# Decoder step with split float32 weights: both parts kept in DRAM after their first use

## The chip, the cores and the metric

The kernel runs on one core of a Trainium2 chip. The metric is the device time of one execution in microseconds (us). TensorE does the matmuls, VectorE (DVE) and ScalarE (ACT) the element-wise work, GpSimd (POOL) a few small operations, and SyncE (SP) issues most DMAs. Every engine works through its own queue in order, and the engines wait for one another through semaphores.

## What is computed

One inference step of a one-layer hybrid decoder on a prompt of 2048 tokens and a sample group of 8 x 8 tokens, model width 1024. Cut to what matters:

```python
h = rmsnorm(x, norm1_g)
z = h @ w_in                                   # 1024 x 4352: r, k, v, low-rank columns, pooling branch, two gates
a = up_a(rwkv7(shifted z))                     # recurrence over tokens, 8 heads x 64
b = up_b(pool(z))                              # causal means over 2, 4, 8, 16 tokens
x = x + (sig(gate_a) * a + sig(gate_b) * b) @ w_o
h = rmsnorm(x, norm2_g)
x = x + square(relu(h @ w_ff1)) @ w_ff2        # 1024 -> 4096 -> 1024
y = rmsnorm(x, final_norm_g)
```

The inputs, the weights and the result are float32; the states of the recurrence, the shift and the pooling are outputs as well.

## The kernel before

**Split products.** A float32 product is made of three float32r matmuls. A weight w is split into hi, its float32r rounding, and lo = w - hi; the activations are split in the same way, and hi x hi, lo x hi and hi x lo are added up in one PSUM tile (`products`).

**Blocks and stages.** The 2112 tokens are cut into five blocks of 384, 448, 448, 448 and 384 columns, the sample group in the fourth. A block goes through three stages: A (the input projection, matmuls named pi and pv), M (the up projections pab and the output projection po) and F (the feed-forward, in 8 groups of 512 hidden columns, named pf and p). The constant ORDER sets how stages of the blocks follow each other: A0 A1 A2 M0 A3 F0 M1 A4 F1 M2 F2 M3 F3 M4 F4. The recurrence runs beside them in 16 sub-steps of 128 tokens (names k0 to k15) and one for the samples (k16): chains of small matmuls, VectorE and GpSimd operations and DMA round trips that are mixed into the matrix work.

**Units of weights.** `load_unit` (line 156) fetches 512 KB of weights, 128 partitions x 1024 values, enough for 24 matmuls. There are 34 units in an A stage, 16 in an M stage and 64 in an F stage (in each group four of w1, then four of w2), 114 a block and 570 in all. A unit has a raw tile (two buffers), and tiles for hi and for lo (three buffers each). SP's queue issues the load into raw (line 164), ScalarE casts raw to hi (166), VectorE subtracts (167). A raw tile is free when VectorE has read it, a hi or lo tile when TensorE has done the unit's last matmul.

In stage F the second product goes in an order of its own: three quarters of w2's first two units, then the last quarters of these, then units three and four. So the unit that takes over the tile of w2's first unit, w2's fourth, follows close behind it: of the 96 matmuls of a group's second product, the first unit's last is number 42 and the fourth unit's first is number 73. In stage M the output projection does the same once: the first unit's last is number 45 and the fourth's first is number 73.

**Order.** TensorE's order is written out: `TensorOrder` chains every matmul to the one before it. The order on the other engines comes from a scheduler at build time, which places the instructions by their dependences and priorities. A queue never overtakes: what waits at its head holds all that is behind it. SP's queue also has at most eight DMAs under way, since a DMA waits for the eighth before it.

**GpSimd** has little: the powers behind the RMS norms (rs, line 181; rt, line 785, from which VectorE makes the tiles md that TensorE needs), the state product of the recurrence (spk, 1283), the group norm's scale (sm), small fills, and the DMAs of the constants in the first 60 us and of the sample states (sld).

Of the kernel before, what the change touches and what calls it, by code (L numbers as in the profile page):

```python
# [12 lines left out]
F32 = mybir.dt.float32  # L13
F32R = mybir.dt.float32r
AF = mybir.ActivationFunctionType
ALU = mybir.AluOpType
# [4 lines left out]
P = 128  # L21
# [46 lines left out]
def hybrid_step(ctx: ExitStack, tc: tile.TileContext, a: dict, outs: list):  # L68
# [11 lines left out]
    V, S, G, D = nc.vector, nc.scalar, nc.gpsimd, nc.sync  # L80

    cp = ctx.enter_context(tc.tile_pool(name="cp", bufs=1))
    dr = ctx.enter_context(tc.tile_pool(name="dr", bufs=1, space=DRAM))
    wp = ctx.enter_context(tc.tile_pool(name="wp", bufs=3))
# [69 lines left out]

    T = TensorOrder()

    def load_unit(parts, shape, name):
        raw = wp.tile([P, 1024], F32, tag="raw", name=name + "r", bufs=2)
        hi = wp.tile([P, 1024], F32R, tag="whi", name=name + "h")
        lo = wp.tile([P, 1024], F32R, tag="wlo", name=name + "l")  # L160
        used = 0
        for src in parts:
            k, n = src.shape[1], src.shape[2]
            D.dma_start(out=raw[:, used:used + k * n].rearrange("p (k n) -> p k n", k=k), in_=src)
            used += k * n
        S.copy(hi[:, :used], raw[:, :used])  # L166
        V.tensor_tensor(lo[:, :used], raw[:, :used], hi[:, :used], op=ALU.subtract)  # L167
        r = lambda t: t[:, :used].rearrange("p (k n) -> p k n", n=shape[1])
        return r(hi), r(lo)

# [136 lines left out]
    for job in h_jobs(0):  # L307
        job()
    dg0 = diagonals(r1_of[0], tok_tiles(0), "r1d0")
    pre = {m: load_unit([w_in[:, :, m * P:(m + 1) * P]], (8, P), f"wi0_{m}") for m in (12, 13)}  # L310

    consts = ExitStack()
# [12 lines left out]
    for dst, vec in ((muv, a["mu_shift"][2 * DA:3 * DA]), (lng, a["ln_x_g"]), (lnb, a["ln_x_b"])):  # L325
        for e in range(2):
            G.dma_start(out=dst[e * 64:e * 64 + 64],
                        in_=vec.rearrange("(q e i) -> e q i", e=2, i=HD)[e].unsqueeze(0).to_broadcast([64, NPAIR, HD]))
# [64 lines left out]
    for e in range(2):  # L393
        G.dma_start(out=vsd[:, 0, e * 256:(e + 1) * 256].rearrange("s (q i) -> s q i", i=HD),
                    in_=a["state_shift"][:, 2 * DA:3 * DA].rearrange("s (q e i) -> e s q i", e=2, i=HD)[e])
# [55 lines left out]
    def col_tile(b, hs, m, evac):  # L451
        g0, n, s = blocks[b]
        wu = (pre.pop(m, None) if b == 0 else None) or load_unit([w_in[:, :, m * P:(m + 1) * P]], (8, P), f"wi{b}_{m}")
        ps = mm_ps(f"pi{b}_{m}")
        yield from gemm(ps[:, :n + s], products(wu, hs, range(8), n + s))
        if b not in rrow:
            h_rows(b, None if b else dg0)
        evac(n + s, ps)
# [38 lines left out]
    def values(b, hs):  # L497
# [5 lines left out]
        for q in range(4):  # L503
            wu = load_unit([w_in[:, 2 * q:2 * q + 2, 2 * DA:3 * DA]], (2, DA), f"wv{b}_{q}")
            for (o, sz, kind, src) in tiles:
                if q == 0:
                    pss[o] = (mm_ps, wk_ps)[len(pss) // 3](f"pv{b}_{o}")
                for kk in range(2):
                    k = 2 * q + kk
                    for i, (x, w) in enumerate(((hs[0], wu[0]), (hs[0], wu[1]), (hs[1], wu[0]))):  # L510
                        T.matmul(pss[o][:sz, :], col(x, k, o, sz), w[:, kk, :], start=(k == 0 and i == 0), stop=(k == 7 and i == 2))
                        yield
# [481 lines left out]
    for i in range(2):  # L994
        t = dr.tile([32, 32, 32], F32, name=f"dxf{i}")
# [511 lines left out]
```

## Time and profile before

| | |
|---|---|
| time, median of 3 runs (lowest to highest) | 3177.41 us (3175.01 to 3185.4) |
| the profiled execution | 3178.24 us |
| its span, first to last instruction | 3176.5 us |
| busy: TensorE, VectorE, ScalarE, GpSimd | 97%, 65%, 40%, 5% |
| granted TensorE clock, mean | 0.99 of 2.4 GHz |
| DMA: moved, mean rate | 462 MB, 146 GB/s |
| DMA queues: share of the DMA engines' time | SP 50.3%, GpSimd 0.2% |

The stages, by the first and last matmul that carries their names, lie at these times of the span: A0 27 to 191 us, A1 to 407, A2 to 617, M0 to 706, A3 to 915, F0 to 1246, M1 to 1343, A4 to 1522, F1 to 1886, M2 to 1982, F2 to 2380, M3 to 2483, F3 to 2815, M4 to 2888, F4 to 3140.

How to read it: a row of the windows view gives a stretch's length, and for each engine the busy time and in brackets its instructions; PEclk is the clock that TensorE was granted, 1.00 for 2.4 GHz and 0.50 for 1.2 GHz; then the mean busy share of the 16 DMA engines and what they moved. A row of the waits view names an engine and its instruction, and behind the arrow what ended its wait. Idle time of an engine that is not the bound costs nothing.

### The profile page before, as it was taken

Reading aid. Unit: us, or ns where it says so; the run is one execution under the profiler, and the core shown is the slowest. Engines: PE = TensorE matmul, PEld = TensorE weight load, DVE = VectorE, ACT = ScalarE, POOL = GpSimd, SP = SyncE. Lnnn points to the kernel's source line nnn. Section 1 sums busy time; section 2 is a strip of 40 time slices with the busy share of each in tenths; the row PEclk is TensorE's granted clock in tenths of the full one; section 3 lists DMA queues with packets and bytes.
Section 4 is the critical chain, followed back from the end, with each engine's and each line's share of the span. In section 5 each row is a group of like instructions: output and inputs, shape, how many; then the busy total and the mean of one; then the engine's idle time right before and its main releaser. Section 6 shows DMA issues by size and latency. Waiting matters only on the chain.

```text
span 3176.5 us, 55187 instructions
## 1 busy us (share of the span) xinstructions
PE 3077.0 (97%) x21869; PEld 2816.8 (89%) x21869; DVE 2060.8 (65%) x3992; ACT 1256.4 (40%) x2108; POOL 158.8 (5%) x361
## 2 busy tenths in 40 slices
PE   7999999899999999999999999999999999999997
PEld 7898888888899999898988889888898899999997
DVE  5757666586748667775757668557668654466554
ACT  5444433353333434543443434333334333344333
POOL 4000000000100000010000000000001000000000
PEclk9999999999999999999999999999999999999999
DMA  7756665564544455655544356334446444364443
GB/s 219 204 155 177 187 173 147 152 164 134 146 133 130 127 144 160 200 166 145 159 118 116 114 146 183 102 89 130 125 118 198 108 122 121 107 209 133 120 133 106
DMA packets 738662, 462.24 MB, mean 146 GB/s; under 512 B 143649, under 2 KB 715467, under 8 KB 738396
## 3 DMA queue, kind: packets, MB, share of 16 engines
q1 hardware_dynamic: 737476, 457.55, 50.3%
q8 instruction: 172, 2.82, 0.4%
q0 software_dynamic: 928, 1.16, 0.2%
q14 instruction: 86, 0.70, 0.1%
HBM read 388.81 MB, written 65.54 MB: 143 GB/s over the span
## 4 chain that ended last, share of the span: by engine, by line
PE 76%; DVE 9%; DMA 8%; issue 2%; SPq 2%; ACT 2%; POOL 1%; DVEq 0%; POOLq 0%; ACTq 0%
PE pf L150 20%; PE p L150 20%; PE pi L150 16%; PE po L150 5%; PE pab L150 3%; PE pv L150 3%; DMA pin<-pd 1%; DMA gm<-gd 1%; DMA lin<-zd 1%; SPq L1171 0%; PE gT L150 0%; DVE acc L914 0%; SPq L1167 0%; PE k16py L150 0%; DMA out<-xo 0%
## 5 line engine op out<-in xcount | busy, mean ns | idle before, releaser
L914 DVE TENSOR_TENSOR acc<-p,acc 128x448 f32<-128x448 f32 (+1 forms) x320 | 181.1, 591 | 164.2 <-PE p L150 163.7
L852 DVE SCALAR_TENSOR_TENSOR rl<-pf,rsc 128x448 f32<-128x448 f32 (+1 forms) x160 | 94.8, 594 | 163.7 <-PE pf L150 162.8
L166 ACT CAST w_3h<-w_3r 128x1024 fp32r<-128x1024 f32 x80 | 84.1, 1051 | 284.7 <-PE p L150 150.0
L166 ACT CAST w_1h<-w_1r 128x1024 fp32r<-128x1024 f32 x80 | 84.0, 1050 | 234.3 <-DMA w_1r<-in_w_ff 102.9
L166 ACT CAST w_2h<-w_2r 128x1024 fp32r<-128x1024 f32 x80 | 84.0, 1050 | 160.0 <-PE pf L150 81.3
L167 DVE TENSOR_TENSOR w_1l<-w_1r,w_1h 128x1024 fp32r<-128x1024 f32 x80 | 97.8, 1222 | 58.8 <-ACT w_1h L166 58.6
L166 ACT CAST w_0h<-w_0r 128x1024 fp32r<-128x1024 f32 x80 | 84.2, 1052 | 102.0 <-PE pf L150 75.8
L150 PE MATMUL p<-gh,w_2h 128*128 128x448 f32 (+1 forms) x320 | 114.9, 359 | 8.6 <-DVE acc L914 8.6
L150 PE MATMUL p<-gh,w_1h 128*128 128x448 f32 (+1 forms) x320 | 114.0, 356 | 2.2 <-ACT gs L717 2.2
L150 PE MATMUL p<-gh,w_0h 128*128 128x448 f32 (+1 forms) x320 | 114.3, 357 | 0.3 <-ACT gh L855 0.3
L150 PE MATMUL p<-gl,w_2h 128*128 128x448 f32 (+1 forms) x320 | 114.3, 357 | 0.0
L150 PE MATMUL p<-gh,w_2l 128*128 128x448 f32 (+1 forms) x320 | 114.1, 356 | 0.0
L150 PE MATMUL p<-gl,w_3h 128*128 128x448 f32 (+1 forms) x320 | 113.5, 355 | 0.0
L150 PE MATMUL p<-gh,w_3h 128*128 128x448 f32 (+1 forms) x320 | 113.5, 355 | 0.0
L150 PE MATMUL p<-gh,w_3l 128*128 128x448 f32 (+1 forms) x320 | 113.4, 354 | 0.0
L150 PE MATMUL p<-gh,w_1l 128*128 128x448 f32 (+1 forms) x320 | 113.3, 354 | 0.0
L150 PE MATMUL p<-gh,w_0l 128*128 128x448 f32 (+1 forms) x320 | 113.0, 353 | 0.0
L150 PE MATMUL p<-gl,w_1h 128*128 128x448 f32 (+1 forms) x320 | 112.9, 353 | 0.0
L167 DVE TENSOR_TENSOR w_2l<-w_2r,w_2h 128x1024 fp32r<-128x1024 f32 x80 | 97.7, 1222 | 22.5 <-ACT w_2h L166 22.2
L150 PE MATMUL p<-gl,w_0h 128*128 128x448 f32 (+1 forms) x320 | 107.1, 355 | 3.9 <-DVE gl L857 3.9
L167 DVE TENSOR_TENSOR w_3l<-w_3r,w_3h 128x1024 fp32r<-128x1024 f32 x80 | 97.5, 1219 | 17.6 <-ACT w_3h L166 17.6
L167 DVE TENSOR_TENSOR w_0l<-w_0r,w_0h 128x1024 fp32r<-128x1024 f32 x80 | 97.6, 1220 | 13.8 <-ACT w_0h L166 13.5
(3861 smaller groups left out, 9810.5 us busy)
## 6 DMA issues: line engine op xcount, KB each, us to landing
w_0r<-in_w_ff SPq DMA_DIRECT2D x80, 512.0 KB
w_1r<-in_w_ff SPq DMA_DIRECT2D x80, 512.0 KB
w_2r<-in_w_ff SPq DMA_DIRECT2D x80, 512.0 KB
w_3r<-in_w_ff SPq DMA_DIRECT2D x80, 512.0 KB
gd<-gt SPq DMA_DIRECT2D x48, 224.0 KB
gm<-gd SPq DMA_DIRECT2D x48, 224.0 KB
gf<-in_final_norm_g SPq DMA_DIRECT2D x36, 256.0 KB
out<-xo SPq DMA_DIRECT2D x15, 512.0 KB
```

The source lines that it names most:

```text
L150: self.issue(nc.tensor.matmul(out, lhsT, rhs, start=start, stop=stop), cost)
L166: S.copy(hi[:, :used], raw[:, :used])
L167: V.tensor_tensor(lo[:, :used], raw[:, :used], hi[:, :used], op=ALU.subtract)
L852: V.scalar_tensor_tensor(rl[:, :nt], ps[:, :nt], 0.0, rs, op0=ALU.max, op1=ALU.mult)
L914: V.tensor_tensor(acc[:, m, :nt], pss[m][:, :nt], acc[:, m, :nt], op=ALU.add)
```

## The change

`load_unit` keeps a table, `split`, of units that it has met. The key is the unit's name without its block number, so all five blocks share an entry. At a unit's first use (all 114 units of block 0) the load and the split stay, and two DMAs on SP's queue write hi and lo to two new DRAM tensors, 128 rows of 4 KB each. For the 456 units of the later four blocks, nothing is cast or subtracted and no raw tile is taken: GpSimd's queue loads hi and lo from those DRAM tensors straight into the tiles, two DMAs of 512 KB. The DRAM tensors are float32 and the tiles float32r, so these loads convert the type.

```diff
+    split = {}
+
     def load_unit(parts, shape, name):
-        raw = wp.tile([P, 1024], F32, tag="raw", name=name + "r", bufs=2)
+
+        key = name.split("_", 1)[1] + name[:2]
         hi = wp.tile([P, 1024], F32R, tag="whi", name=name + "h")
         lo = wp.tile([P, 1024], F32R, tag="wlo", name=name + "l")
-        used = 0
-        for src in parts:
-            k, n = src.shape[1], src.shape[2]
-            D.dma_start(out=raw[:, used:used + k * n].rearrange("p (k n) -> p k n", k=k), in_=src)
-            used += k * n
-        S.copy(hi[:, :used], raw[:, :used])
-        V.tensor_tensor(lo[:, :used], raw[:, :used], hi[:, :used], op=ALU.subtract)
+        used = sum(src.shape[1] * src.shape[2] for src in parts)
+        both = [(hi, "h"), (lo, "l")]
+        if key in split:
+            for (t, x), d in zip(both, split[key]):
+                G.dma_start(out=t[:, :used], in_=d)
+        else:
+            raw, o = wp.tile([P, 1024], F32, tag="raw", name=name + "r", bufs=2), 0
+            for src in parts:
+                k, n = src.shape[1], src.shape[2]
+                D.dma_start(out=raw[:, o:o + k * n].rearrange("p (k n) -> p k n", k=k), in_=src)
+                o += k * n
+            S.copy(hi[:, :used], raw[:, :used])
+            V.tensor_tensor(lo[:, :used], raw[:, :used], hi[:, :used], op=ALU.subtract)
+            split[key] = [dr.tile([P, used], F32, name=f"wd{name}{x}") for _, x in both]
+            for (t, x), d in zip(both, split[key]):
+                D.dma_start(out=d, in_=t[:, :used].bitcast(F32))
         r = lambda t: t[:, :used].rearrange("p (k n) -> p k n", n=shape[1])
         return r(hi), r(lo)
```

TensorE's rows are the same before and after. VectorE has 3644 rows before and 3188 after. Three places on the queues:

SP's queue early in A0, before (wi_0r is the raw tile of the input projection's columns 0 to 127, xd and zd are activations on their way to DRAM):

```order
L215 DMA xd_110<-n_0_0c_203 128x4x128
L164 DMA wi_0r<-in_w_in 128x8x128
L215 DMA xd_110<-n_0_128c_219 128x4x128
L164 DMA wi_1r<-in_w_in 128x8x128
L215 DMA xd_110<-n_0_256c_235 128x4x128
L752 DMA acc_6301<-xd_110 128x8x384
L164 DMA wi_2r<-in_w_in 128x8x128
L164 DMA wi_3r<-in_w_in 128x8x128
L164 DMA wi_4r<-in_w_in 128x8x128
```

The same place after (wdwi_0h and wdwi_0l are the new DRAM tensors of that unit):

```order
L227 DMA xd_110<-n_0_256c_235 128x4x128
L179 DMA wdwi_0h<-wi_0h 128x1024
L179 DMA wdwi_0l<-wi_0l 128x1024
L173 DMA wi_2r<-in_w_in 128x8x128
L764 DMA acc_6305<-xd_110 128x8x384
L179 DMA wdwi_1h<-wi_1h 128x1024
L179 DMA wdwi_1l<-wi_1l 128x1024
L173 DMA wi_3r<-in_w_in 128x8x128
L179 DMA wdwi_2h<-wi_2h 128x1024
L179 DMA wdwi_2l<-wi_2l 128x1024
L173 DMA wi_4r<-in_w_in 128x8x128
```

The load of raw tile i + 2 now follows both writes of unit i, whose raw tile it takes over.

GpSimd's queue at the beginning of F2, before (rt are the powers of block 2's second norm, k16am and k16rm fills for the sample group's recurrence):

```order
L785 TENSOR_TENSOR rt_20557<-rt_20557,mhalf 128x1 x3
L785 TENSOR_TENSOR rt_20557<-rt_20557,mhalf 64x1
L1352 MEMSET k16am_21007 128x512
L1352 MEMSET k16rm_21008 128x512
L1352 MEMSET k16am_21228 128x512
```

The same place after, where w_0_3 is the fourth unit of w1 in F2's first group and w_0_0 the first of w2:

```order
L168 DMA w_0_3h<-wdw_0_3h 128x1024
L797 TENSOR_TENSOR rt_20529<-rt_20529,mhalf 128x1 x3
L797 TENSOR_TENSOR rt_20529<-rt_20529,mhalf 64x1
L168 DMA w_0_0l<-wdw_0_0l 128x1024
L168 DMA w_0_0h<-wdw_0_0h 128x1024
```

The powers and fills now stand between loads, each of which waits until TensorE has freed its tile.

GpSimd's queue a little later in F2, after, with full names (w22_1_3h is hi of block 2, w2, group 1, fourth unit; before, none of these rows of loads is on GpSimd):

```order
L168 DMA w22_1_2l_21278<-wdw20_1_2l_10258 128x1024
L168 DMA w22_1_2h_21277<-wdw20_1_2h_10257 128x1024
L1364 MEMSET k16am1_21176 128x512
L1364 MEMSET k16rm1_21177 128x512
L168 DMA w22_1_3l_21326<-wdw20_1_3l_10323 128x1024
L168 DMA w22_1_3h_21325<-wdw20_1_3h_10322 128x1024
L168 DMA w12_2_0l_21433<-wdw10_2_0l_10393 128x1024
```

Both parts of a unit are loaded one behind the other, lo first, and the next unit's loads follow.

## Rows read from the trace of the kernel before

**Rows 1.** The page, part 1: busy us, share of the span, instructions
```profile
PE 3077.0 (97%) x21869; PEld 2816.8 (89%) x21869; DVE 2060.8 (65%) x3992; ACT 1256.4 (40%) x2108; POOL 158.8 (5%) x361
```

**Rows 2.** The page, part 5: the cast and the subtraction, one of four each
```profile
L166 ACT CAST w_3h<-w_3r 128x1024 fp32r<-128x1024 f32 x80 | 84.1, 1051 | 284.7 <-PE p L150 150.0
...
L167 DVE TENSOR_TENSOR w_1l<-w_1r,w_1h 128x1024 fp32r<-128x1024 f32 x80 | 97.8, 1222 | 58.8 <-ACT w_1h L166 58.6
```

**Rows 3.** Waits of TensorE, 100 to 3140 us: total us, times, longest
```profile
PE mr L150 <- DVE md L188: 9.2, 2, 4.8
PE p L150 <- DVE acc L914: 8.6, 8, 2.2
PE gT L150 <- DVE lin L707: 8.1, 1, 8.1
...
PE sput L153 <- POOL us L577: 3.1, 1, 3.1
...
PE wpt L153 <- DMA wpl<-in_w_pool: 0.2, 1, 0.2
```

**Rows 4.** Windows: A0, A1, M0, F0, M1, M4, F4; last PEclk, DMA share, GB/s
```profile
27.00:191.00 164.00, 157.37 (x896) 150.66 (x897) 105.70 (x242) 72.87 (x135) 30.26 (x135) 0.96 0.72 196
191.00:407.00 216.00, 212.71 (x1708) 183.63 (x1708) 140.47 (x293) 99.50 (x200) 12.34 (x20) 1.00 0.61 174
617.00:706.00 89.00, 86.95 (x825) 81.57 (x826) 69.60 (x138) 48.37 (x104) 6.36 (x11) 1.00 0.59 163
915.00:1246.00 331.00, 322.44 (x2760) 308.30 (x2760) 225.84 (x406) 133.24 (x218) 12.96 (x23) 1.00 0.48 135
1246.00:1343.00 97.00, 91.66 (x623) 81.78 (x622) 79.60 (x172) 48.52 (x98) 4.67 (x7) 1.00 0.70 208
2815.00:2888.00 73.00, 70.58 (x415) 69.31 (x414) 51.56 (x85) 36.57 (x62) 3.08 (x4) 1.00 0.68 215
2888.00:3140.00 252.00, 252.00 (x1460) 252.00 (x1459) 133.63 (x189) 93.83 (x126) 2.45 (x3) 1.00 0.43 128
```

**Rows 5.** Windows: two stretches of 2 us in the crowded start
```profile
20.00:22.00 2.00, 2.00 (x8) 2.00 (x7) 0.12 (x1) 2.00 (x8) 0.00 (x0) 0.50 1.15 345
4.00:6.00 2.00, 0.43 (x2) 0.46 (x3) 0.65 (x1) 0.81 (x2) 1.88 (x6) 1.00 1.02 398
```

**Rows 6.** The chain in order of time: start, us, what; 384, then 448 columns
```profile
1017.49 16.64 PE p L150 x96
...
1730.86 19.46 PE p L150 x96
```

**Rows 7.** The chain in F0: one turn of a raw tile
```profile
952.93 4.45 DMA w_1r<-in_w_ff
...
957.46 1.05 ACT w_1h L166
...
958.53 1.24 DVE w_1l L167
```

**Rows 8.** Timeline in F4: start, us, engine, line, operation, idle before it
```profile
3014.14 1.05 ACT L166 CAST w_3h<-w_3r 128x1024 fp32r<-128x1024 f32 x1 [5.25 <-PE p L150]
...
3019.14 0.33 PE L150 MATMUL p<-gh,w_3h 128*128 128x384 f32 x1
```

**Rows 9.** DMA issues on GpSimd's queue: times, KB each, median us to landing
```profile
sld<-in_state_pool POOLq DMA_DIRECT2D x1, 240.0 KB, 3.7
...
lng<-in_ln_x_g POOLq DMA_DIRECT2D x2, 64.0 KB, 7.4
...
sld<-in_state_shift POOLq DMA_DIRECT2D x2, 16.0 KB, 2.3
```

**Rows 10.** Tiles rt, sld and w_1r: duration in ns, least, median, most
```profile
L785 POOL TENSOR_TENSOR rt<-rt,mhalf x18: 530/542/2674, 803.6 to 2898.0; 128x1 f32<-128x1 f32 x15, 64x1 f32<-64x1 f32 x3
L643 POOL DMA_DIRECT2D sld<-in_state_shift x3: 502/537/567, 138.1 to 153.8; - x3
L164 SPq DMA_DIRECT2D w_1r<-in_w_ff x80: 367/372/672, 903.6 to 3130.1; - x80
```

## The prediction, made before the result was known

> **What bounds the kernel now.** I read the page's busy line first. TensorE is busy 97% of the span; VectorE, ScalarE and GpSimd are busy 65%, 40% and 5% [rows 1]. The two engines that the change relieves are not the bound: 456 casts and 456 subtractions leave the program, about 479 and 557 us of busy time [rows 2], and none of it can come back except as time in which TensorE stands still. Next I read who TensorE waited for between 100 and 3140 us [rows 3]: 25 rows, from 9.2 down to 0.2 us, 61.5 us in all. VectorE ends 51.0 of them, ScalarE 6.5, GpSimd 3.1, DMAs the rest. So 58 us, 1.8%, is the ceiling of any gain.
>
> Then the stages [rows 4]: window, busy times, granted clock, DMA share, GB/s. The clock is at its upper level, 2.4 GHz, almost throughout. The DMA column is what the change leans on: 196 GB/s in A0, 163 in M0, 135 in F0, the three stages in which every weight is used first. Where DMA runs flat out [rows 5] the core moves 345 GB/s, 398 in the best two microseconds. In bare matrix work 24 matmuls, one unit of weights, take 4.16 us at 384 columns and 4.87 at 448 [rows 6].
>
> **The change part by part.** A unit is 512 KB, so 0.524 MB for each part and 1.05 MB for both. There are 114 units a block, 34 in A, 16 in M, 64 in F.
>
> *First use, bytes.* Each of the 114 units now also writes 1.05 MB to DRAM on SP's queue. A0 moves 164 us x 196 GB/s = 32.1 MB today and gets 34 x 1.05 = 35.7 more. 67.8 MB take 196 us at 345 GB/s and 170 at 398, against 164: +6 to +32. Up to three units' writes (9 us) can trail into A1, which has room (174 GB/s) [rows 4, 5]. Bounds 0 and 32; I take **17**. M0: 14.5 + 16.8 = 31.3 MB, 91 us at 345 against 89: **2** (0 to 10). Its two first raw tiles are loaded long before.
>
> *First use, the turn of the two raw tiles.* F0's bytes just fit: 44.7 + 67.1 = 111.8 MB, 324 us of 331. But on SP the next raw load now stands behind both writes of the unit whose raw tile it takes (the order shows it). The chain of waits shows the turn today: DMA 4.45 us, cast 1.05, subtraction 1.24 [rows 7], 6.7 us for two tiles, 3.4 a unit, which the 4.16 hide. With 1.05 MB ahead of it (3.0 us at 345 GB/s) and one more issue on SP (0.4 [rows 10]) it is 10.2, or 5.1 a unit. Against the bare pace that costs 64 x 0.9 = 60 us, against F0's mean of 331/64 = 5.17, with the recurrence in between, nothing. I take a third, **20**.
>
> *Later loads.* The cast and the subtraction stood between a raw tile that had landed early and a part tile that came free late. Now the whole transfer stands there: a part tile must be free before its load may start. With three tiles for each part that leaves two units, 8.3 to 9.7 us, except once in each group of F: w2's fourth unit takes the tile of w2's first, whose last matmul comes only 30 matmuls ahead of its use. In F4 the cast shows the tile free at 3014.14, and TensorE needs the unit at 3019.14: 5.0 us [rows 8], hence 6.0 at 448 columns. What the load takes, no row shows, for none of GpSimd's DMAs is that large. The nearest is its 16 KB load with 2.3 us from issue to landing [rows 9]; add 1.05 MB at the rate of F4 itself, 128 GB/s at a share of 0.43 [rows 4], 298 GB/s, 3.5 us: 5.8 for the pair. That is late by 0.8 in F4's 8 groups and in time in the other 24: **7**. At 345 GB/s it would be 8 x 0.3 = 2. The upper bound is GpSimd's own 240 KB load in A0: 1.4 us more than the small ones for 224 KB more, 160 GB/s, so 8.9 us for the pair: 8 x 3.9 + 24 x 2.9 = 101 [rows 9]. I stay with F4's rate, since it is the stage in question and its DMA share is 0.43, not 0.72. W_o has one such place for each of M1 to M4 (27 matmuls): **2** (0 to 16).
>
> The Trainium skill ("DMA: Bandwidth & Descriptors", Anatomy of one DMA) gives a GpSimd-issued DMA about 2.0 us plus its bytes at 436 GB/s. By that a pair takes about 4.4 us, an estimate, every place is in time, and the sum would be 9 us lower. The small loads' 2.3 us agrees with its fixed part; the 7.4 us for 64 KB in the crowded first 35 us does not [rows 9].
>
> The load changes type, float32 to float32r, so it is a converting DMA. No row shows one; a slower conversion is the second rival.
>
> *GpSimd's order.* 912 loads join an engine that carries the recurrence's state products, the group norm's scale and the RMS norms' powers. An issue takes 0.54 us there [rows 10], two a unit, 1.1 of 4.2 to 4.9: no bound by itself. But a load that waits for its tile holds what is behind it, at most until TensorE ends a unit: the state product of 17 sub-steps, for which the next chunk's VectorE add waits, and the powers in front of md, for which TensorE already waits 9.2 us [rows 3]. The other way round, a power that waits for VectorE holds the next loads. Mostly 2 to 3 us of slack cover this: **8** (0 to 25).
>
> *DMA in the later stages.* 0.524 MB more a unit. M4 goes from 215 to (15.7 + 8.4)/73 = 330 GB/s, close to the 345; M1 to 295; A1 to 256 [rows 4]. The loads that feed the recurrence get slower: **5** (0 to 25).
>
> *The gain.* Of the 58 us, 8.1 wait for lin [rows 3], which follows a DMA's round trip, and 10.6 lie in M0 and F0 (89 less 87.0 busy, 331 less 322.4 [rows 4]), where the splits stay. Of the remaining 38 half go away at once; the other half are the engine's own chains (md, the recurrence), for which less load is not enough. **-19** (-58 to 0).
>
> Sum: 17 + 2 + 20 + 7 + 2 + 8 + 5 - 19 = +42. The profiled execution took 3178.24 us (span 3176.5 and 1.7 around it), 0.8 above the median of 3177.41. 3178.24 + 42 - 0.8 = 3219.
>
> **The rivals.** *Faster.* First use is hidden: A0's writes run at 398 GB/s and trail, and F0's turn hides in the recurrence. The late places are met. Then the 38 us come back less 5 for GpSimd's order: 3145. For it: DMA shares of 0.43 to 0.70 in the later stages, beside 1.15 in the crowded start [rows 4, 5]. Against it: A0's 0.72 before any write is added.
>
> *The queue is slower than pace.* If GpSimd's converting loads run at 160 GB/s, a pair needs 6.55 us. The span without 27 us ahead of A0, without A0, M0 and F0, and without 36 us behind F4 holds 456 units: (3176 - 27 - 164 - 89 - 331 - 36)/456 = 5.55 us each [rows 4], so every unit is 1.0 late: 456 beside the 42 above, 3675. It decides from 189 GB/s down. For it: the 240 KB row and the missing price of a conversion. Against it: A0's other traffic slowed that row.
>
> *VectorE holds GpSimd up.* A one-element power on GpSimd takes 0.54 us in the median and 2.67 at most [rows 10]. If issues are held like that while VectorE works, a pair lands 4.3 us later, at 10.1: the late places cost 8 x 5.1 + 24 x 4.1 + 19 = 158, with the other terms +191: 3368. Against it: three issues in A0, with VectorE busy 64% of the stage, took 0.50 to 0.57 [rows 4, 10]. The Trainium skill ("SBUF — State Buffer", the box on DVE blocking DMA) states just this, that GpSimd cannot write descriptors while VectorE runs a two-port mode; the 2.67 us agrees with it for an operation, no row here shows it for a DMA.
>
> *Nothing to measure.* Gain and cost within 10 us of each other: 3177. That the change doesn't do what it says is excluded by the order: VectorE has 456 rows fewer, TensorE the same rows.
>
> **How the numbers follow.** About 0.3%, 10 us, is what a measurement of this kernel can tell from no change. Chances: forecast 0.48, faster 0.20, nothing 0.12, slow queue 0.13, GpSimd held up 0.07. So faster 0.20, same 0.12, slower 0.68. The forecast's own range is 3187 to 3330 (first use near its upper bounds, some late loads). The range for all goes from 3150, which leaves out half of the faster case, to 3400, which leaves out most of the slow queue: about 0.2 outside.
>
> **What would show it.** A0 longer by 10 to 30 us with a DMA share near 1, F0 longer with ScalarE's cast waiting for raw loads; A1 to A4 no longer than now. In F4 matmuls with w_3h wait for GpSimd's DMA by about 1 us, 8 times. TensorE's waits for md and acc halve. Wrong would be: F1 to F4 longer by tens of us each (the queue), GpSimd issues of over 1 us (held up), or A0 and F0 unchanged (first use free).

## The result and the profile after

The changed kernel takes 3284.32 us in the median of four runs (3282.5 to 3287.57), beside 3177.38 for the kernel before in the same session: a ratio of 1.0333, interval 1.0313 to 1.0354. The forecast was 3219. The way was right and the time lies inside the range, but the change costs 107 us where 42 were forecast.

Page of the changed kernel, part 1 (busy us, share of the span, instructions):

```profile
span 3280.8 us, 55177 instructions
PE 3113.6 (95%) x21869; PEld 2838.2 (87%) x21869; DVE 1564.9 (48%) x3536; ACT 805.5 (25%) x1652; POOL 631.9 (19%) x1273
```

Beside [rows 1], VectorE lost 496 us of work and ScalarE 451, and the program is no shorter for it. TensorE runs the same 21,869 matmuls, yet it is busy 36.6 us longer. The rest of the 104 us by which the span grew, 67.7, is time in which it stands still. Two things are therefore to be found: the waits, and why the same matmuls took longer.

Where they lie is seen by stage. TensorE's row is the same in both kernels (28 matmuls of the recurrence's sub-steps 6 and 7 stand in another order among themselves), so a stage begins at the same matmul number in every trace, and its length can be compared. Windows of the stages A0, A1, M0, F0, M4 and F4 of the changed kernel, columns as in [rows 4]:

```profile
24.90:220.10 195.20, 164.16 (x896) 153.18 (x897) 107.97 (x241) 72.36 (x135) 29.77 (x136) 0.93 1.02 341
220.10:461.30 241.20, 221.67 (x1710) 190.30 (x1709) 102.76 (x260) 67.92 (x166) 47.57 (x88) 0.95 0.79 237
...
674.80:765.70 90.90, 88.35 (x825) 82.90 (x826) 68.85 (x137) 46.73 (x103) 8.63 (x15) 0.98 0.91 300
...
965.00:1315.50 350.50, 331.89 (x2760) 315.47 (x2759) 228.88 (x411) 132.41 (x217) 14.45 (x27) 0.97 0.95 314
...
2906.20:2989.40 83.20, 73.17 (x415) 71.95 (x414) 34.60 (x69) 20.75 (x46) 19.51 (x36) 0.94 0.87 288
2989.40:3243.80 254.40, 253.72 (x1459) 251.73 (x1459) 66.62 (x128) 33.82 (x65) 65.16 (x123) 1.00 0.79 251
```

A0 and F0, where the parts are written, are 32 and 20 us longer, with the DMA engines full. (A0 also begins 2.6 us earlier, so it ends 29 us later.) A1, where nothing is written and the first reloads run, is 25 longer at a DMA share of only 0.79. M4 is 10 longer. The waits of TensorE over the whole program say what came late ([rows 3] left out the first 100 us). In the kernel before:

```profile
PE pi L150 <- DVE zr L478: 3.4, 1, 3.4
...
PE pab L150 <- DVE gm L804: 1.0, 2, 0.8
```

In the changed kernel:

```profile
PE pab L150 <- DVE gm L816: 14.3, 5, 8.7
PE pi L150 <- DVE zr L490: 11.4, 1, 11.4
PE k2psd L150 <- DMA k2wd<-in_w_decay: 8.2, 1, 8.2
...
PE p L150 <- ACT w_1h L175: 5.1, 1, 5.1
...
PE mr L150 <- DVE md L200: 5.0, 2, 3.9
...
PE pf L150 <- DVE w_1l L176: 4.1, 3, 2.6
...
PE p L150 <- DMA w_3h<-wdw_3h: 3.7, 6, 1.7
...
PE po L150 <- DMA wo_3h<-wdwo_3h: 1.9, 2, 1.1
```

The first three are new or larger, and each hangs on a transfer that is not one of the reloads. k2wd is a small load of the recurrence, the one of in_w_decay for chunk 2. gm is M's gate, loaded from gd. The zr of A0 stands behind a raw weight load, shown below. The reloaded tiles themselves make TensorE wait little: 3.7 us for w_3h, 1.9 for wo_3h, 1.7 for w_1h.

### The profile page after: what moved, and what is told of

Same layout as the page of the kernel before. It is cut to its first block, busy times and chain, and to the rows that moved or that the text cites. A ratio compares the mean times of both kernels' runs of the same rounds, so it can differ in the third digit from the quotient of the medians.

```text
span 3280.8 us, 55177 instructions
## 1 busy us (share of the span) xinstructions
PE 3113.6 (95%) x21869; PEld 2838.2 (87%) x21869; DVE 1564.9 (48%) x3536; ACT 805.5 (25%) x1652; POOL 631.9 (19%) x1273
## 4 chain that ended last, share of the span: by engine, by line
PE 55%; DMA 16%; issue 14%; DVE 6%; SPq 3%; POOL 3%; ACT 2%; POOLq 0%; DVEq 0%; ACTq 0%
PE pi L150 14%; PE pf L150 13%; PE p L150 12%; PE pab L150 3%; PE pv L150 3%; PE po L150 2%; DMA gm<-gd 1%; DMA w_3h<-wdw_3h 1%; DMA w_0r<-in_w_ff 1%; DMA wbd<-wbf 1%; SPq L179 1%; DMA wbf<-in_w_b_up 1%; DMA zd<-zs 1%; DMA w_1r<-in_w_ff 1%; SPq L1183 0%
## 5 line engine op out<-in xcount | busy, mean ns | idle before, releaser
L867 ACT ACTIVATE gh<-rl 128x448 fp32r<-128x448 f32 (+1 forms) x160 | 88.9, 557 | 720.4 <-DVE rl L864 720.4
L869 DVE TENSOR_TENSOR gl<-rl,gh 128x448 fp32r<-128x448 f32 (+1 forms) x160 | 95.3, 596 | 117.8 <-ACT rl L868 117.4
L475 DVE TENSOR_TENSOR gt<-pi,rs 128x448 f32<-128x448 f32 (+1 forms) x80 | 47.4, 592 | 111.4 <-PE pi L150 91.5
L481 ACT ACTIVATE gt<-gt 128x448 f32<-128x448 f32 (+1 forms) x80 | 44.5, 556 | 225.5 <-DVE gt L475 195.7
L168 POOL DMA_DIRECT2D w_3l<-wdw_3l x64 | 34.5, 540 | 333.4 <-PE p L150 197.2
L868 ACT ACTIVATE rl<-rl 128x448 f32<-128x448 f32 (+1 forms) x160 | 88.6, 556 | 4.2
L168 POOL DMA_DIRECT2D w_1l<-wdw_1l x64 | 34.5, 540 | 266.9 <-PE pf L150 127.8
L168 POOL DMA_DIRECT2D w_2l<-wdw_2l x64 | 34.5, 540 | 254.6 <-PE pf L150 128.9
```

Of the source, the lines that this page charges most:

```text
L168: G.dma_start(out=t[:, :used], in_=d)
L475: V.tensor_tensor(dst, ps[:, :sz], rrow[b][:, :sz], op=ALU.mult)
L481: S.activation(gt[:, :n + s], gt[:, :n + s], AF.Tanh, scale=0.5)
L867: S.activation(gh[f][:, :nt], rl[:, :nt], AF.Square)
L868: S.activation(rl[:, :nt], rl[:, :nt], AF.Square)
L869: V.tensor_tensor(gl[f][:, :nt], rl[:, :nt], gh[f][:, :nt], op=ALU.subtract)
```

## Experiments

Each kernel is the changed kernel with the edit shown, unless the text says otherwise; ratios are to the kernel before, run on the same chip beside it. Differences of a stage to the kernel before, in us, read from one profile of each run by matmul number. M1, A4, M3 and F3 are left out; they differ by less than 5 us each. The last line runs from the span's start to the end of F4:

| Stage | before | after | w_only | r_only | r_sp | a_sp | sel |
|---|---|---|---|---|---|---|---|
| A0 | 163.5 | +31.7 | +32.3 | +3.2 | +30.0 | +27.5 | -0.1 |
| A1 | 216.2 | +25.0 | +1.8 | +29.7 | +5.8 | +8.2 | -0.3 |
| A2 | 210.6 | +2.9 | -2.3 | -3.5 | +3.3 | +3.1 | -1.3 |
| M0 | 88.3 | +2.6 | +5.0 | +1.4 | +4.1 | +2.5 | +1.2 |
| A3 | 209.0 | -9.7 | +0.1 | -14.8 | -12.4 | -12.5 | -10.5 |
| F0 | 331.1 | +19.5 | +20.3 | +0.4 | +22.4 | +19.9 | +1.6 |
| F1, M2, F2 | 858.1 | +19.9 | -0.8 | +26.1 | +4.9 | +19.1 | -1.0 |
| M4 | 73.0 | +10.2 | +0.2 | +10.1 | +5.6 | +9.7 | -0.1 |
| F4 | 252.0 | +2.4 | 0.0 | +2.5 | 0.0 | +7.5 | 0.0 |
| start to end of F4 | | +103.8 | +52.1 | +51.2 | +55.2 | +87.7 | -12.2 |

**Which half of the change costs? w_only and r_only.** In w_only the parts are written and nobody reads them:

```diff
-        if key in split:
+        if False:
...
-            split[key] = [dr.tile(...) ...]          # and the two writes
+            if key not in split: ...                 # the same, at the first use only
```

> The first use writes both parts to DRAM as in the changed kernel; the later blocks load the raw weights and split them as the kernel before does, so nothing reads what was written. Theory A (the first use carries its own cost and no more): A0 +32 us, M0 +3, F0 +20 as in the trace after, every other stage within 5 us of before: about 3232 us, ratio 1.017. Theory B (the first use's writes also trail into A1 and make its 25 us): 3257, ratio 1.025. Theory C (A0 and F0 only grow because of what the reloads do to the tiles and the queue): under 3200.

It took 3233.11 us, ratio 1.0171 (1.0152 to 1.019). In r_only all later units reload, but from eight stored pairs only:

```diff
+            if len(kept) < 8:
+                kept.append(...)                     # and the two writes
-            split[key] = [dr.tile(...) ...]
+            split[key] = [d[:, :used] for d in kept[len(split) % len(kept)]]
```

> Only the first eight units write their parts (16 DMAs in place of 228); the later blocks reload as in the changed kernel, each unit from one of these eight pairs, so the weights of the later blocks are the wrong ones while bytes, shapes and queues are those of the changed kernel. Theory A (two separate costs that add): 3284 - 55 = 3229 us, ratio 1.016, with A1 longer by about 25 us, M4 by 10, F1 to F4 by 19 together, A3 shorter by 10, A0 and F0 within 5 us of before. Theory B (A1 is long from trailing writes): 3204, ratio 1.008. Theory C (the reloads give the gain that was forecast, and the first use alone costs): under 3177.

It took 3230.03 us, ratio 1.0159 (1.0144 to 1.0174). Theory A held in both: +56 and +52 add up to 108, beside the 107 of the change, and in the table each stage shows mainly the one cost or the other, though the two do not add up in every stage (A1: 1.8 and 29.7, together 25.0). A1's 25 us come from the reloads; no write trails into it.

**The first use: bytes or order? w_half and w_gp.** Both are w_only with a changed write. w_half writes the lo part alone; w_gp issues the writes on GpSimd's queue.

```diff
-            for (t, x), d in zip(both, split[key]):
+            for (t, x), d in list(zip(both, split[key]))[1:]:         # w_half
-                D.dma_start(out=d, in_=t[:, :used].bitcast(F32))
+                G.dma_start(out=d, in_=t[:, :used].bitcast(F32))      # w_gp
```

> The first use alone, as in w_only, but only the lo part of each unit is written: half the bytes. Theory bytes against a ceiling of about 345 GB/s: A0 moves 32.1 + 17.9 = 50 MB, 145 us of its 164, and F0's turn is one write shorter, 8.6 us for two tiles or 4.3 a unit, under F0's 5.17: both within 5 us of before, 3182 us in all, ratio 1.0015. If each write costs by itself (issue, tile held), half of the 55 us stays: 3205, ratio 1.009.

> The first use alone, as in w_only, but its writes are issued on GpSimd's queue, so that SP's raw loads no longer stand behind them. If F0's 20 us come from that order on SP (the turn of the two raw tiles), F0 falls back to within 5 us of before while A0 keeps its 32: 3217 us, ratio 1.0125. If they come from the bytes (F0 moved 314 GB/s at a share of 0.95), nothing changes: 3233 within 5, ratio 1.017.

w_half took 3194.13 us, ratio 1.005 (1.0031 to 1.0069): with half the bytes 15 us stay of w_only's 56, A0 +8, F0 +7. That is 12 us above the time that a mere ceiling gives and 11 below that of a cost for each write: the cost falls faster than the bytes, but does not end below the ceiling. w_gp took 3266.17, ratio 1.0276 (1.0253 to 1.0299): 31 us more than w_only, each against the kernel before beside it, which neither theory had. Off SP's queue the writes no longer hold the raw loads, and F0's waits for w_1h and w_1l are gone; but A0 grew by 42 and M0 by 15, and F0, still 28 longer, now waits for the recurrence and for acc instead. Freed of SP's order the same bytes cost more. How much of F0's 20 us that order makes, this run cannot tell, since another cost took its place.

What a full DMA path does to one load is seen in A0 of the changed kernel. Timeline of SP's queue (start, us, engine, line, operation), and under it the chain's piece that follows from its last row:

```profile
34.47 0.53 SPq L179 DMA_DIRECT2D wdwi_1l<-wi_1l  x1
35.05 0.55 SPq L173 DMA_DIRECT2D wi_3r<-in_w_in  x1
```

```profile
35.05 11.14 DMA wi_3r<-in_w_in
...
47.42 1.23 DVE wi_3l L176
48.65 0.48 DVE zr L475
```

The raw load of unit 3, issued straight behind the two writes of unit 1, lands 11.1 us later, and the subtraction that waits for it stands in front of zr in VectorE's row: the wait of 11.4 us above (3.4 in the kernel before).

**The reloads: which property of the queue? r_sp, r_nc, g_free.** r_sp moves the later loads to SP's queue, as plain float32; r_nc leaves them on GpSimd's without the conversion; g_free keeps them as they are and moves six lines of the recurrence from GpSimd to VectorE.

```diff
-                G.dma_start(out=t[:, :used], in_=d)
+                D.dma_start(out=t[:, :used].bitcast(F32), in_=d)      # r_sp
+                G.dma_start(out=t[:, :used].bitcast(F32), in_=d)      # r_nc
```

```diff
-            G.tensor_tensor(spk, spk, PC, op=ALU.mult)
+            V.tensor_tensor(spk, spk, PC, op=ALU.mult)                # g_free, one of six
```

> The changed kernel with its later loads on SP's queue, as plain float32 copies into the same tiles; everything else as it is. If the reloads' cost is in their bytes, the time is that of the changed kernel, 3284, within 10 us. If it is in GpSimd's order and queue (loads held behind a power, powers held behind a load), 3240 to 3265. If a load that waits for its tile holds the recurrence's own small loads behind it on SP's queue, 3320 or more, with A1 to A4 longer still.

> The changed kernel with its later loads on GpSimd's queue as before, but float32 to float32: no conversion in the DMA. If the conversion costs nothing, 3284 within 10 us and the same median of 4.0 to 5.4 us from issue to landing. If it slows the loads, 3255 or less and landings shorter by half a microsecond or more.

> The changed kernel with the recurrence's work of GpSimd (two memsets, the copy, the state product, the two scales of the group norm, six lines in all) moved to VectorE, which is busy 48% there; only the powers stay between the loads. If GpSimd's order (a load held behind such a step, a step held behind a load) makes A1 and the other stages long, 3265 or less. If it is what the loads do on the DMA engines, 3284 within 10 us and A1 still longer than before by 20 or more.

r_nc took 3277.51 us, ratio 1.032 (1.0281 to 1.0358), not to be told from the changed kernel: the conversion costs nothing here that shows. g_free took 3287.42, ratio 1.0347 (1.0333 to 1.0361), with A1 still 22 us longer: the six steps of the recurrence between the loads in GpSimd's row cost nothing either. The powers stayed between them. r_sp took 3233.82, ratio 1.0179 (1.0163 to 1.0194), as much as the writes alone. The same bytes on SP's queue cost the later stages next to nothing; on GpSimd's they cost 50 us. This lies 6 us under the range given for GpSimd's order and queue. Of the order, g_free clears the six steps; the powers no run takes out, but TensorE's wait for md, which follows them, fell from 9.2 us to 5.0 [rows 3].

What differs is what happens to the smaller loads on SP's queue. The chain of waits in order of time (start, us, what) has k2wd's load from issue to landing. In the changed kernel:

```profile
412.15 11.98 DMA k2wd<-in_w_decay
```

In g_free:

```profile
411.78 11.96 DMA k2wd<-in_w_decay
```

In r_sp:

```profile
406.19 5.14 DMA k2wd<-in_w_decay
```

Twelve us where the reloads run on GpSimd's queue, five where they run on SP's. What a load waits before it is issued is not in these times; the stages' lengths have it. The timeline of GpSimd in the changed kernel shows what flew beside the load:

```profile
409.93 0.55 POOL L168 DMA_DIRECT2D wi_30h<-wdwi_30h  x1
...
412.66 0.60 POOL L168 DMA_DIRECT2D wi_31l<-wdwi_31l  x1 [1.88 <-PE pi L150]
413.27 0.55 POOL L168 DMA_DIRECT2D wi_31h<-wdwi_31h  x1
```

wi_31's megabyte was issued after k2wd and was moved along with it. On SP's queue such loads stand behind k2wd and are moved after it. The DMA view of the time from issue to landing gives for each queue its packets, MB and share of the DMA engines' time (packets overlap, so shares can pass 100%). In the changed kernel, where software_dynamic is GpSimd's queue and hardware_dynamic SP's:

```profile
q1 hardware_dynamic: 1782, 1.49, 52.8%
q0 software_dynamic: 518, 1.86, 51.2%
```

In r_sp:

```profile
q1 hardware_dynamic: 1726, 1.44, 107.2%
```

The rate is 282 GB/s both times, and SP's queue moved nearly the same bytes until the load had landed; the changed kernel moved 1.86 MB of reloads beside them, with about half of the engines' time. The Trainium skill ("DMA: Bandwidth & Descriptors", Queues, rings and completion order) says that each DMA engine takes turns between the queues that have work, a packet at a time. The two shares near a half agree with that.

M4 shows the same thing. Timeline of VectorE there, with the wait before the row in brackets, the row of SP's queue with the load that ended this wait, and the two queues from its issue to its landing:

```profile
2948.16 0.56 DVE L816 SCALAR_TENSOR_TENSOR gm<-gm,pab 128x384 f32<-128x384 f32 x1 [9.34 <-DMA gm<-gd]
```

```profile
2930.34 3.97 SPq L813 DMA_DIRECT2D gm<-gd  x2
```

```profile
q0 software_dynamic: 1057, 3.84, 59.1%
q1 hardware_dynamic: 1784, 3.05, 50.8%
```

The gate's load was issued at 2930.3, behind SP's own 1.5 MB load of acc, and landed at 2947.7, 17.4 us later; the reloads of W_o and of the last up projections took more than half of the engines' time, at 398 GB/s in all. TensorE waited 8.7 us. In r_sp the first gate load behind acc's took 9.9 us, at the same 398 GB/s:

```profile
q1 hardware_dynamic: 1968, 3.97, 105.3%
```

There it is a reload that comes late, in its turn on SP's queue. TensorE's longest wait in M4 of r_sp:

```profile
PE pab L150 <- DMA wab_6h<-wdwab_6h: 4.7, 1, 4.7
```

k2wd's load and this one of gm are the worst cases. Other loads of in_w_decay, as far as their landing shows, take 5 to 9 us in the changed kernel and 6 to 8 in r_sp, and VectorE's waits for gm's loads add up to 27.2 us and 25.4. But TensorE stands still for 37 us less in r_sp, and most of this is theirs: 14.3 us of waits for gm against none, 13.3 for in_w_decay against 2.8.

**Bytes alone, and a second queue of another engine: d_gp, d_sp, a_sp, a_act.** d_gp and d_sp are the kernel before; its later units write their hi part to DRAM as well, so that the later blocks move the changed kernel's bytes and no matmul waits for the extra ones.

```diff
         V.tensor_tensor(lo[:, :used], raw[:, :used], hi[:, :used], op=ALU.subtract)
+        if name.split("_")[0][-1] != "0":
+            more = dr.tile([P, used], F32, name=f"wd{name}")
+            G.dma_start(out=more, in_=hi[:, :used].bitcast(F32))      # d_gp; D in d_sp
```

> The kernel before, with 0.52 MB more for each of the 456 later units: its hi part is written to DRAM on GpSimd's queue, where nothing waits for it. Bytes in the later blocks are then those of the changed kernel, but no matmul waits for a transfer on GpSimd's queue. If large transfers on a second queue share the DMA engines with the recurrence's small loads and delay them, A1, F1, M2, F2 and M4 grow as in r_only, by 40 us or more together: 3215 or more. If r_only's cost lies in the waits of GpSimd's own order or of the tiles, this stays under 3190.

> As d_gp, the same extra bytes, but on SP's queue, in one line with the small loads. If a shared queue is what keeps r_sp cheap, the later stages grow by under 15 us together: under 3192. If the bytes cost the same on either queue, the same time as d_gp within 10 us.

d_gp took 3221.74 us, ratio 1.0129 (1.0101 to 1.0157), d_sp 3199.99, ratio 1.0069 (1.0054 to 1.0084). Both are partial: GpSimd's queue doubles the cost of the same bytes and d_gp came out over its 3215, but the five stages named grew by 31 us and not 40; on SP's queue the bytes cost 21 us where under 15 were expected; and in A1 there was no difference at all (+7 and +8). The doubling comes above all from F1 (+14 and +4) and A3 (+5 and -4). A1's 25 us thus need more than bytes on that queue. In the changed kernel the two loads of a unit are issued together as soon as a matmul frees their tiles, in d_gp one write follows each cast; that this is the difference was not tried.

a_sp puts the reloads of the A units alone on SP's queue; a_act is r_sp with those of the A units on ScalarE's queue.

```diff
-                G.dma_start(out=t[:, :used], in_=d)
+                (D if name[:2] in ("wi", "wv") else G).dma_start(...)   # a_sp
+                (S if name[:2] in ("wi", "wv") else D).dma_start(...)   # a_act
```

> The changed kernel with the later loads of the A units alone on SP's queue (plain float32), those of M and F still on GpSimd's. If the queue costs where the recurrence's small loads run beside it, A1 falls from +25 to +6 us against before and A3 and A4 shorten by 2 each, the rest stays as in the changed kernel: 3260. If A1's 25 us are the bytes of A1, 3284 within 5.

> The changed kernel with every later load a plain float32 copy on SP's queue as in r_sp, but those of the A units on ScalarE's queue: a second queue again beside the recurrence's small loads, and not GpSimd's. If any second queue takes the small loads' place in the line, the load of in_w_decay for k2 in A1 takes 9 us or more from issue to landing (12.0 in the changed kernel, 5.1 in r_sp), A1 is longer than before by 15 or more, and the whole takes 3245 or more. If it is GpSimd's queue alone, that load takes 7 us or less. A long A1 with a short load would be ScalarE's own order: a load that waits for its tile holds evictions.

a_sp took 3271.65 us, ratio 1.0298 (1.0282 to 1.0314). A1 fell from +25 to +8 as expected, with A1's own bytes unchanged, and k2wd's load took 6.2 us there; 13 us of the expected 24 arrived, in part because F3 and F4 came out 2.5 and 5 longer than in the changed kernel. a_act took 3242.59, ratio 1.0201 (1.0181 to 1.0221), 2 us under the bound for "any second queue", with A1 at +21. But its load took

```profile
413.07 6.82 DMA k2wd<-in_w_decay
```

6.8 us, under the bound set for "GpSimd's queue alone". In these 6.8 us ScalarE's queue (q10) moved 0.56 MB beside SP's 1.35, since a_act's next reloads were issued some 3 us behind the load (about 1 in the changed kernel):

```profile
q1 hardware_dynamic: 1650, 1.35, 72.9%
q10 hardware_dynamic: 152, 0.56, 33.0%
```

So the load was short where little flew beside it, which does not clear a second queue of another engine. Nor is A1 shown to be long from ScalarE's own order. TensorE waits most for ScalarE's work, k1XB:

```profile
PE k1p L150 <- ACT k1XB L1233: 5.5, 1, 5.5
```

But ScalarE's row there stands idle until another smaller load of SP's queue, wbf, has landed:

```profile
385.91 0.61 ACT L613 ACTIVATE wbf<-wbf,pscale 128x384 f32<-128x384 f32 x1 [7.97 <-DMA wbf<-in_w_b_up]
```

At the same place it is idle for 10.0 us in the changed kernel and 8.1 in r_sp. What makes A1 long in a_act, and whether any second queue does what GpSimd's does, therefore stays open. What is shown: the 50 us come with the reloads on GpSimd's queue and go with them on SP's, at the same bytes; the conversion is not the reason, nor are the six steps that g_free moved; and in the two worst waits the late load shared the engines with those reloads. That this sharing makes all of the 50 us is argued, not shown: r_sp also issues its reloads at other times, in the order of SP's row, and no run tells the two apart.

**A kernel that keeps the gain: sel.** The only stage that got much shorter is A3. sel is made of that: the last 18 of A's 34 units are written in A2 and reloaded in A3 on SP's queue, and everything else is the kernel before.

```diff
-        if key in split:
+        if blk == 3 and key in split:
...
-            split[key] = [dr.tile(...) ...]
+            if blk == 2 and kind and seen[blk] > 16:                  # then as in the change
```

> The kernel before, with the reload only where a gain was seen: the last 18 of A's 34 units write their parts in A2 (18.9 MB more there, 253 GB/s in all) and are reloaded in A3 on SP's queue; all other units, blocks and stages load and split as before. If the gain of 10 to 15 us in A3 comes from the splits that VectorE and ScalarE no longer do beside the recurrence, A3 is 10 or more shorter and A2 within 4: 3165, ratio 0.996. If it needs the whole chain of stages, or A2's writes cost as A0's did, 3177 or more.

It took 3167.04 us, ratio 0.9965 (0.9953 to 0.9978), 11 us faster than the kernel before and the fastest of all. A3 is 10.5 us shorter, A2 1.3. The waits of the kernel before in A3 (the third is in [rows 3]):

```profile
PE pi L150 <- DVE h3l L214: 5.0, 1, 5.0
PE mr L150 <- DVE md L188: 4.4, 1, 4.4
PE sput L153 <- POOL us L577: 3.1, 1, 3.1
```

The waits of sel there:

```profile
PE pi L150 <- DVE h3l L229: 4.4, 1, 4.4
PE mr L150 <- DVE md L203: 1.0, 1, 1.0
```

So 7.1 of 12.5 us of waits are gone, and 3.4 us of TensorE's busy time with them.

## Why the forecast was right in its way and too small in its size

| Term | forecast | measured |
|---|---|---|
| A0's writes | 17 (0 to 32) | 31.7; in w_only 32.3 |
| M0 | 2 (0 to 10) | 2.6 |
| F0 | 20 (0 to 60) | 19.5 |
| late tiles of w2 and W_o | 9 (2 to 117) | 7.8 of waits for w_3h, w_1h, wo_3h and wab_5h |
| GpSimd's order | 8 (0 to 25) | none seen (g_free, six of the steps) |
| more DMA in the later stages | 5 (0 to 25) | 48.6 (changed kernel less r_sp, last line of the stages) |
| gain | -19 (-58 to 0) | -10 in A3, -2 in M1 |
| TensorE's clock | not in the sum | +36.6 of busy time, inside the rows above |

**The first use.** 39 were forecast, 56 measured. The byte count was right: A0 ran at 341 GB/s against the 345 of [rows 5], and 67.8 MB by 345 is the 196 us that it took. The step that failed here was to choose the middle between 345 and 398 GB/s and to let writes trail into A1. Stretches reach 398 (17 us in M4, above), but no whole stage does; the upper bound, 32, was what came. F0's size was right. Its reason is borne out in part: TensorE waits there 12.5 us for w_1h and w_1l, whose raw loads stood behind the writes. But w_gp takes them out of that line and pays 28 us, so it is not told apart from F0's bytes, 314 GB/s at a share of 0.95.

**The later loads, tile by tile.** Here the forecast held best. A pair was to take 5.8 us; the page gives for F's units 4.0 to 5.4 from issue to landing, the second of a pair issued 0.5 after the first:

```profile
w_3l<-wdw_3l POOLq DMA_DIRECT2D x64, 512.0 KB, 4.0
w_3h<-wdw_3h POOLq DMA_DIRECT2D x64, 512.0 KB, 4.8
```

so a pair takes 5.3 to 5.9. That the sum came out, 7.8 us beside 9, is in part luck: in F4 w_3h was late by 0.5 us in all, not 6, and 3.2 us of its waits lie in F1 to F3, where it was to be in time. The rival of a slow queue falls with these rows and with r_nc. So does the one in which VectorE holds GpSimd up:

```profile
L168 POOL DMA_DIRECT2D w_1l<-wdw_1l x64: 527/534/617, 1586.8 to 3239.6; - x64
```

No issue of the 64 took over 0.62 us, and none of all 912 over 0.65. The Trainium skill ("SBUF — State Buffer", the box on DVE blocking DMA) describes such a block; with VectorE busy 48% of the span, these rows show none.

**The later loads, everything else.** This is the term that failed: "DMA in the later stages", 5 us, at most 25. The forecast looked at whether the reloads would be late and at whether the bytes fit (they do: A1 moved 237 GB/s), and gave the smaller loads beside them a token. It had A1 to A4 no longer than before; A1 became 25 us longer. Apart from the writes the later stages were to cost 3 us net, and on SP's queue they cost 1 (r_sp less w_only). On GpSimd's queue it was 52 (r_only). One load of 5 us became one of 12 in A1, and the gate of M4 kept VectorE waiting 9.3, although over these stages the DMA engines were not full (shares of 0.79 and 0.87).

**The clock.** The sum counted waits alone. Behind such a wait TensorE was granted half its clock for a while, and the same matmuls take longer. Windows of A1 ahead of the wait for k2wd (416.2 to 424.4), just behind it, and later:

```profile
400.00:416.00 16.00, 16.00 (x123) 13.93 (x117) 4.49 (x9) 4.37 (x10) 5.03 (x8) 1.00 0.72 219
425.00:432.00 7.00, 7.00 (x25) 6.09 (x25) 4.11 (x10) 3.40 (x9) 1.58 (x4) 0.50 0.13 28
433.00:441.00 8.00, 8.00 (x40) 7.32 (x40) 7.78 (x13) 1.87 (x5) 1.19 (x3) 1.00 1.05 308
```

These windows hold different matmuls. The same eight, k2psa, stand in the chain of the changed kernel, and in that of r_sp, where the clock there was 1.00:

```profile
426.43 1.71 PE k2psa L150 x8
```

```profile
412.70 0.89 PE k2psa L150 x8
```

Over the span the granted clock fell from 0.990 to 0.978, and TensorE's busy time rose by 36.6 us beside 67.7 us of new waits. By the first part of their pages w_only's longer span has 32 us of waits and 20 of busy time in it, r_only's 32 and 19. By that share the 42 us of the forecast, all of them waits, would have been about 65. In A3 the gain has it too: 6.6 us of waits and 3.1 of busy time came back.

**The gain.** The forecast named 38 us that could come back (58 less 8.1 and 10.6 is 39) and took half. About 12 did, 10 of them in A3, beside its recurrence; M1's 2 are not seen in r_only. The waits for md and acc, which were to halve, went from 9.2 to 5.0 us and from 8.6 to 7.4. Where VectorE's splits delay nothing that is late, their removal, 496 us of busy time in all, was worth nothing.

## What to carry to other kernels

Before a load is moved to another queue, ask which small loads its old queue served in order: here the large transfers, once on a second queue, were moved along with smaller loads issued before them, and it was these that came late. With both on one queue the large ones waited their turn, and some of them came late instead, at less cost. A stage whose bytes come near the rate that a whole stage sustains is costed at that rate (here 341 GB/s in A0), not at the best short stretch. A wait is costed with what the clock adds behind it, here about half as much again, and relief for an engine that is not the bound is bought only where the trace shows TensorE waiting for it, as sel does with 18 units of one stage.

## What was not expected of the hardware

- One small load of the recurrence took 12.0 us from issue to landing beside 0.5 MB loads on GpSimd's queue and 5.1 us with the same loads on its own queue, while its own queue moved 1.49 and 1.44 MB and the engines 282 GB/s both times.
- Writing 0.12 GB on GpSimd's queue instead of SP's cost 31 us more (w_gp against w_only), although nothing reads what is written.
- A converting load of 512 KB on GpSimd's queue landed in 4.0 to 5.4 us, and one without conversion in 3.9 to 5.6: the program's times differ by less than their intervals (1.0313 to 1.0354 and 1.0281 to 1.0358).
- TensorE's busy time for the same 21,869 matmuls varied from 3077 to 3117 us between these kernels. Busy time times mean granted clock is the same before and after (3077.0 x 0.990 and 3113.6 x 0.978), so there the clock accounts for it.
